# MLP of a two-layer hybrid decoder: the second half of its first part as seven block products

## The chip, the cores and the metric

The kernel runs on one core of one Trainium2 chip. The metric is the device time of one execution in microseconds (us). Before the change the median of three runs is 1323.62 us (1322.04 to 1324.94). All times below are of that core; the engines are TensorE (PE, with its weight loads as PEld), VectorE (DVE), ScalarE (ACT), GpSimd (POOL) and SyncE (SP, which issues most transfers).

## The reference, cut to what matters

Two layers over 512 tokens of width 1024. Each layer has a mixer (attention and an mLSTM, merged and projected by `w_out`) and then an MLP:

```python
def hybrid_layer(x, ..., w_out, norm_ffn, w_ff1, w_ff2):
    ...
    x = x + mixed @ w_out
    u = jax.nn.relu(rmsnorm(x, norm_ffn) @ w_ff1)      # w_ff1: 1024 x 4096
    return x + (u * u) @ w_ff2                         # w_ff2: 4096 x 1024
```

All arrays are float32. The kernel keeps that accuracy by splitting every operand of a large product into a high part `h` (float32 rounded to the matmul's fp32r form, one ACT instruction) and a low part `l` (the rest, one DVE instruction). A product is then three matmuls: high by high, high by low, low by high (`mm3`). The mean square of the norm is not multiplied into the activations but into the MLP's result, so the MLP can begin before the norm's factor is known.

## The kernel before, in words

**Parts.** The MLP's 4096 hidden columns are worked off in four parts. Part p takes the columns 512p to 512p+511 of the lower 2048 and the same of the upper 2048. Within a part, i = 0 and i = 1 take 256 columns each of both (n = 0 lower, n = 1 upper). For every part the first matrix gives `u`, and `second` multiplies it by rows of `w_ff2`.

**Two ways to form `u`.** Parts 1 to 3 use `first`: the activations are cut into four blocks (two halves of the 1024 inputs, two halves of the 512 tokens), the weights into four (two halves of the inputs, n = 0 and 1), and the 2x2 block product is formed with seven block products instead of eight, from sums and differences of blocks. The seven are numbered 1 to 7 and stand in the order 5, 1, 3, 6, 2, 7, 4. One block product is 4 x 2 x 3 = 24 matmuls of 128x128 by 128x256. Its results are copied, added and put through ReLU and square by `copy` (line 1139) and `finish` (lines 1143 to 1145), and the products share banks of PSUM: 5, 3 in one half of the pair of banks "f", 1, 6, 7 in the other half, 2 and 4 in the two small buffers `aux` that the transposes use too. Part 0 uses `Plain`: an ordinary product for each i and n, 8 x 2 x 3 = 48 matmuls of 128x128 by 128x512.

**Differences of the activations.** `left_blocks` forms the sums of high and low again and from them the differences that products 5, 6, 3 and 7 need, splits them and keeps them for all parts (`hs`, and for 7 in the place of a block that is no longer needed, `late`).

**Sums of the weights.** Products 5, 6 and 4 run on growing sums of blocks of `w_ff1`. The buffer `p` is loaded by SP (`w1_load`, line 946) and the next block is added into it by a transfer that accumulates, which only POOL issues (`w1_add`, line 951): one such addition before product 5, one between 5 and 6, one between 6 and 4. Buffer `q` serves 3 and then, after one addition, 7; buffer `r` serves 1 and is loaded anew for 2. Each product's weights are split by `w_split` (ACT line 910, DVE line 911) into one of five pairs of buffers (`SPL = 5`), so a split has to wait until the product five places earlier is done.

**What sets the order.** Each engine works off its own queue in order. The queues are filled by a scheduling layer, which takes the program's order, the marks `high_priority` and `issue_after` and its own picture of durations, and which may put matmuls of one product ahead of another's. `weave` lays side work (transposes of `x`, `norm.turn`, and so on) under a list of matmul groups. While the last product of the mixer runs (`w_out`, splits at lines 192 and 193, additions to `x` at line 879), the MLP's first weights are loaded and split. The transposes of `x` use the two `aux` buffers in turn; each is emptied by ACT (line 207) and DVE (line 208).

Of the kernel before, what the change touches and what calls it, by code (L numbers as in the profile page):

```python
# [35 lines left out]
def hybrid_kernel(ctx, tc, x, norm_mix, w_in, att_q_norm, att_k_norm, att_sinks, m_gate_bias,  # L36
# [25 lines left out]
    def nm(s):  # L62
        uid[0] += 1
        return f"{s}_{uid[0]}"
# [29 lines left out]
    def f32(ap):  # L94
        return ap.bitcast(F32)
# [25 lines left out]
    def g_mix(l, k):  # L121
        return gcol[:, 8 * l + k:8 * l + k + 1]
# [132 lines left out]
    def weave(fill, side=()):  # L255

        side = sorted(side, key=lambda e: e[0])
        at = 0.0
        for width, f in fill:
            while side and side[0][0] <= at + 1e-6:  # L260
                side.pop(0)[1]()
            f()
            at += width
        for _, f in side:
            f()
# [76 lines left out]
    norm = norm0 = Norm(lambda k: g_mix(0, k))  # L342
# [25 lines left out]
    def halves_of(dt=F32):  # L368

        return [half.tile([P, 4, T], dt, tag=f"u{g}", name=nm("u")) for g in range(2)]  # L370
# [515 lines left out]
    def mlp(l, norm, late, phase):  # L886
# [31 lines left out]
        def plus(d, p, q):  # L918
            with tc.high_priority():
                ve.tensor_tensor(d, p, q, op=ALU.add)  # L920
# [8 lines left out]
        def new_u(part):  # L929
            if part % 2:  # L930
                return halves_of()
            return [uraw.tile([P, 4, T], F32, tag=f"u{g}", name=nm("u")) for g in range(2)]
# [24 lines left out]
        starts = []  # L957
# [102 lines left out]
        def left_blocks(temps):  # L1060

            ih, il = norm.big
            views = [t[:, :, H * n:H * (n + 1)] for t in temps for n in range(2)]

            def block(t, k):
                kk, c = slice(4 * k, 4 * k + 4), slice(H * t, H * (t + 1))
                return ih[:, kk, c], il[:, kk, c]

            def whole(r, t, k):
                hi, lo = block(t, k)
                plus(r, f32(hi), f32(lo))
                return r

            def keep(which, r):
                with tc.high_priority():
                    lefts[which] = pieces(r, *(hs.tile([P, 4, H], F32R, tag=f"{n}{which}", name=nm("hs")) for n in "hl"))

            def late():  # L1080
                with tc.high_priority():
                    lefts[7] = pieces(r21, *block(1, 0))

            for which, (t, k) in ((1, (0, 0)), (2, (0, 1)), (4, (1, 1))):
                lefts[which] = block(t, k)
            r22, r12, r11, r21 = views
            whole(r21, 1, 0)
            whole(r22, 1, 1)
            minus(r22, r22, r21)
            keep(5, r22)  # L1090
            whole(r11, 0, 0)
            minus(r22, r22, r11, -1.0)
            keep(6, r22)
            whole(r12, 0, 1)
            minus(r12, r22, r12, -1.0)
            keep(3, r12)
            minus(r21, r11, r21)
            return late

        def first(part, i, u):  # L1100

            c0 = T * part + H * i
            ps = {}

            r = {}

            def load(tag, k, n):
                r[tag] = w1_load(tag, k, n, c0)

            def start():  # L1110
                load("p", 0, 0)
                w1_add(r["p"], 0, 1, c0)

            starts.append(start)

            def weights(which):
                tag = {1: "r", 2: "r", 3: "q", 7: "q"}.get(which, "p")
                if which == 1:
                    load("r", 0, 0)
                elif which == 3:  # L1120
                    load("q", 1, 1)
                elif which == 2:
                    load("r", 1, 0)
                    if starts:
                        starts.pop(0)()
                w = w_split(r[tag])
                more = {5: (1, 1), 6: (1, 0), 3: (0, 1)}.get(which)
                if more:
                    w1_add(r[tag], *more, c0)
                return w  # L1130

            def to(t, n):
                return u[i][:, 2 * n:2 * n + 2, H * t:H * (t + 1)]

            def of(b):
                return ps[b].rearrange("p (m t) -> p m t", m=2)

            def copy(t, n, b):
                sc.activation(to(t, n), of(b), AF.Copy)  # L1139

            def finish(t, n, b):
                z = to(t, n)
                ve.tensor_tensor(z, z, of(b), op=ALU.add)
                sc.activation(z, z, AF.Relu, scale=-1.0 if n else 1.0)
                sc.activation(z, z, AF.Square)

            def slot(which, bank, fresh, *done):

                ws = []

                def run():
                    if fresh:
                        if which == 5:
                            two = banks("f")
                            ps["a"], ps["b"] = two[:, 0, :], two[:, 1, :]
                        elif bank in "cd":
                            ps[bank] = aux()
                    (hi, lo), (ah, al) = ws[0], lefts[which]
                    for m in range(2):
                        c = slice(m * P, (m + 1) * P)  # L1160
                        for kt in range(4):
                            mm3(ps[bank][:, H * m:H * (m + 1)], hi[:, kt, c], lo[:, kt, c], ah[:, kt, :], al[:, kt, :],
                                fresh and m + kt == 0, False, skip_group_check=True)

                def end():
                    with tc.high_priority():
                        for f, t, n in done:
                            f(t, n, bank)

                return Slot([lambda: ws.append(weights(which))], [run], end)  # L1170

            return [slot(5, "b", True, (copy, 1, 1)), slot(1, "a", True, (copy, 0, 0)),
                    slot(3, "b", False, (copy, 0, 1)), slot(6, "a", False, (finish, 0, 1)),
                    slot(2, "c", True, (finish, 0, 0)), slot(7, "a", False, (finish, 1, 1), (copy, 1, 0)),
                    slot(4, "d", True, (finish, 1, 0))]

        class Plain:
# [5 lines left out]
            def load(self, h):  # L1183
                r = w1_load("prpq"[2 * h + self.n], h, self.n, self.i * H)
                self.w[h] = w_split(r)
                if self.i + self.n + h == 3:
                    starts.pop(0)()

            def step(self, k):
                if k == 0:  # L1190
# [9 lines left out]
                    sc.activation(dst, self.ps, AF.Relu)  # L1200
                    sc.activation(dst, dst, AF.Square)

            def slot(self, u):
                return Slot([lambda: self.load(0), lambda: self.load(1)],
                            [lambda h=h: [self.step(k) for k in range(4 * h, 4 * h + 4)] for h in range(2)],
                            lambda: self.evac(u))

        us = [new_u(0)]
        plain = [Plain(0, 0, "f"), Plain(0, 1, "x")]
        for h in range(2):  # L1210
            for f in plain:
                f.load(h)
        weave([(0.5, lambda k=k, f=f: f.step(k)) for k in range(KT) for f in plain],
              late + [(6.5, norm.inverse)])
        for f in plain:
            f.evac(us[0])
        us.append(new_u(1))
        slots = [Plain(1, 0, "y").slot(us[0]), Plain(1, 1, "f").slot(us[0])]
        lates = []
        slots[0].before = lambda: lates.append(left_blocks(us[1]))  # L1220
        for part in range(4):
            nxt = []
            if part < 3:
                if part:
                    us.append(new_u(part + 1))
                nxt = first(part + 1, 0, us[part + 1]) + first(part + 1, 1, us[part + 1])
            two = second(part, us[part])
            if part == 0:
                before = two[1].before
                two[1].before = lambda: (lates.pop()(), before())  # L1230
            for s, n in zip(two, (2, 2, 2, 2, 3, 3, 0)):
                slots += [s] + nxt[:n]
                nxt = nxt[n:]
# [8 lines left out]
        def go(i, s, n):  # L1242
# [16 lines left out]
    late = ([(0.75 + 0.9 * (k - 2), lambda k=k: norm.turn(k)) for k in range(2, KT)]  # L1259
            + [(6.5, lambda: gains(grow, 16))]  # L1260
            + [(3.0 + 2.0 * j, lambda j=j: norm.squares(j)) for j in range(2)])
    order = None
    for l in range(DEPTH):
        with ExitStack() as phase:
            norm = mixer(l, norm, late, order, phase)
        late = norm.steps(1, 1.5, 0.5)
        with ExitStack() as phase:
            norm = mlp(l, norm, late, phase)
        late = norm.steps(0, 1.5, 0.5) if norm else []
# [41 lines left out]
```

## Time and profile before

| | us |
|---|---|
| median of three runs | 1323.62 |
| the profiled execution, whole | 1324.14 |
| its span | 1322.4 |
| PE busy | 1296.7 (98% of the span) |
| DVE busy | 953.9 (72%) |
| ACT busy | 768.4 (58%) |
| POOL busy | 217.9 (16%) |

A row of a timeline reads: start, duration (of all in the row), engine, line, operation, result and operands by the program's names, sizes, count, and in brackets the idle time just ahead and what ended it. Matmuls overlap, so the pace of PE is the distance between starts and not the duration. Rows of DMA show the issue; the time to landing is shown apart. Layer 0's MLP begins at 340.45 us of the span, layer 1's at 994.69 us.

### The profile page before, as it was taken

What the parts mean: (1) busy time and instruction counts of PE and PEld (TensorE: products, weight loads), DVE (VectorE), ACT (ScalarE), POOL (GpSimd) and SP (SyncE); (2) the same over time, 40 slices, a digit from 0 to 9 for tenths busy, and PEclk for the clock granted to TensorE, in tenths of its full rate; (3) what the DMA queues carried; (4) which work ended last, traced back from release to release, by engine and by line L of the source; (5) the groups of instructions that cost most, each with busy time, mean ns of one, the idle gap of its engine ahead of it and who ended that gap; (6) DMA issues with size and microseconds to landing.
All of it is one profiled execution on the core that took longest, in us unless ns stands there. A gap on an engine that the chain in (4) does not pass through costs nothing.

```text
span 1322.4 us, 19224 instructions
## 1 busy us (share of the span) xinstructions
PE 1296.7 (98%) x6966; PEld 1101.0 (83%) x6966; DVE 953.9 (72%) x1493; ACT 768.4 (58%) x1367; POOL 217.9 (16%) x323
## 2 busy tenths in 40 slices
PE   8999999999999999999999999999999999999998
PEld 6877788887889989899788777888888899988987
DVE  4688764466568797978947887645756778879786
ACT  5467765445366655666454687564545566655663
POOL 4422311100001132120005123110000110322100
PEclk9999999999999999999999999999999999999999
DMA  5422236746357989686314222367472589797843
GB/s 152 109 66 75 60 97 153 180 128 218 78 126 187 244 190 236 167 194 194 111 33 120 64 72 64 105 153 174 140 235 66 115 223 251 172 245 149 199 144 128
DMA packets 134400, 192.31 MB, mean 145 GB/s; under 512 B 10264, under 2 KB 71808, under 8 KB 134304
## 3 DMA queue, kind: packets, MB, share of 16 engines
q1 hardware_dynamic: 92768, 135.88, 33.6%
q0 software_dynamic: 33344, 39.98, 19.4%
q10 hardware_dynamic: 8192, 15.21, 3.7%
q8 instruction: 55, 0.90, 0.3%
q14 instruction: 41, 0.34, 0.1%
HBM read 188.95 MB, written 31.46 MB: 167 GB/s over the span
## 4 chain that ended last, share of the span: by engine, by line
PE 48%; DVE 5%; ACT 2%; DMA 2%; issue 1%; DVEq 0%; POOL 0%; SPq 0%; ACTq 0%; POOLq 0%
PE mm L47 42%; PE aux L47 5%; DMA raw<-in_w_ff_dram 1%; PE aux L51 1%; DVE wl L193 1%; DVE wl L911 1%; ACT wh L910 1%; ACT t L652 0%; ACT wh L192 0%; DMA w<-in_w_in_dram 0%; DVE ul L903 0%; DVE x L965 0%; DVE t L639 0%; DVE t L689 0%; DVE t L616 0%
## 5 line engine op out<-in xcount | busy, mean ns | idle before, releaser
L47 PE MATMUL mm<-i,wh 128*128 128x512 f32 (+1 forms) x1280 | 353.6, 362 | 2.2 <-ACT u L1139 2.1
L910 ACT ACTIVATE wh<-raw 128x1024 fp32r<-128x1024 f32 x212 | 223.7, 1056 | 164.5 <-PE mm L47 95.5
L911 DVE TENSOR_TENSOR wl<-raw,wh 128x1024 fp32r<-128x1024 f32 x212 | 257.3, 1220 | 80.1 <-ACT wh L910 79.9
L47 PEld LDWEIGHTS mm<-i,wh 128*128 128x128 f32 x1280 | 224.2, 189 | 36.0 <-ACT u L1139 4.5
L47 PE MATMUL mm<-i,wl 128*128 128x512 f32 (+1 forms) x640 | 230.2, 360 | 0.0
L193 DVE TENSOR_TENSOR wl<-w,wh 128x512 fp32r<-128x512 f32 (+1 forms) x208 | 140.8, 677 | 105.0 <-ACT wh L192 101.2
L192 ACT ACTIVATE wh<-w 128x512 fp32r<-128x512 f32 (+1 forms) x208 | 127.1, 612 | 133.3 <-PE mm L47 99.9
L47 PE MATMUL mm<-wh,ul 128*128 128x512 f32 x448 | 174.8, 390 | 1.1 <-DVE ul L903 1.1
L47 PE MATMUL mm<-wh,uh 128*128 128x512 f32 x448 | 175.1, 391 | 0.0
L47 PE MATMUL mm<-wl,uh 128*128 128x512 f32 x448 | 175.0, 391 | 0.0
L47 PE MATMUL mm<-wh,i 128*128 128x512 f32 (+1 forms) x512 | 149.9, 371 | 0.4 <-ACT wh L192 0.4
L951 POOL DMA_DIRECT2D raw<-in_w_ff_dram x48 | 62.2, 1296 | 522.8 <-DVE wl L911 247.0
L47 PEld LDWEIGHTS mm<-i,wl 128*128 128x128 f32 x640 | 120.9, 189 | 17.6
L47 PE MATMUL mm<-hs,wh 128*128 128x256 f32 x576 | 106.7, 286 | 0.3 <-ACT u L1139 0.3
L47 PEld LDWEIGHTS mm<-wh,i 128*128 128x128 f32 x512 | 92.7, 190 | 16.0 <-ACT wh L192 0.8
L47 PEld LDWEIGHTS mm<-wh,ul 128*128 128x128 f32 x448 | 84.2, 188 | 18.5 <-DVE ul L903 1.6
L47 PEld LDWEIGHTS mm<-wh,uh 128*128 128x128 f32 x448 | 84.3, 188 | 16.4 <-issue 0.2
L47 PEld LDWEIGHTS mm<-wl,uh 128*128 128x128 f32 x448 | 84.3, 188 | 15.7
L47 PEld LDWEIGHTS mm<-hs,wh 128*128 128x128 f32 x576 | 90.1, 191 | 7.5 <-ACT u L1139 6.6
L47 PE MATMUL mm<-wl,i 128*128 128x512 f32 (+1 forms) x256 | 94.8, 370 | 0.0
L965 DVE SCALAR_TENSOR_TENSOR x<-mm,ninv,x 128x512 f32<-128x512 f32 x112 | 80.0, 744 | 16.1 <-PE mm L47 15.6
L47 PE MATMUL mm<-wh,a 128*128 128x512 f32 x256 | 82.1, 394 | 2.3 <-DVE x L879 1.2
(244 smaller groups left out, 2130.5 us busy)
## 6 DMA issues: line engine op xcount, KB each, us to landing
raw<-in_w_ff_dram SPq DMA_DIRECT2D x124, 512.0 KB, 5.1
w<-in_w_in_dram SPq DMA_DIRECT2D x128, 256.0 KB, 2.7
raw<-in_w_ff_dram POOLq DMA_DIRECT2D x48, 512.0 KB, 6.5
sum<-in_w_ff_dram ACTq DMA_DIRECT2D x28, 512.0 KB, 5.0
raw<-sum SPq DMA_DIRECT2D x28, 512.0 KB, 4.2
sum<-in_w_ff_dram POOLq DMA_DIRECT2D x20, 512.0 KB, 6.6
w<-in_w_out_dram SPq DMA_DIRECT2D x32, 256.0 KB, 3.4
w<-in_w_att_branch_dram SPq DMA_DIRECT2D x16, 256.0 KB, 2.6
```

Source lines behind the costliest of these rows:

```text
L47: return nc.tensor.matmul(*args, **kw)
L51: return nc.tensor.transpose(*args)
L192: last_wh[:] = sc.activation(wh[:, :off], raw[:, :off], AF.Copy), wh
L193: ve.tensor_tensor(wl[:, :off], raw[:, :off], f32(wh[:, :off]), op=ALU.subtract)
L910: last_wh[:] = sc.activation(hi, r, AF.Copy), hi[:, 0, :]
L911: ve.tensor_tensor(lo, r, f32(hi), op=ALU.subtract)
L951: nc.gpsimd.dma_start(r, w1_block(k, n, c0), accum_op=ALU.add)
L965: ve.scalar_tensor_tensor(xh[:, i, :], ps[:, i, :], norm.inv[:, 0 if sign > 0 else 1, b:b + 1], xh[:, i, :], op0=ALU.mult, op1=ALU.add)
```

## The change

In part 0 the half i = 0 stays plain, on the banks "x" and "y" instead of "f" and "x". The half i = 1 is formed by `first`, as in parts 1 to 3. `left_blocks` is called within the first half, after the transposes, and its last difference (for product 7) right after that half instead of ahead of a later step of `second`. The start of the first sum of weights is no longer tied to the last plain load: the sum for part 0 starts after the four plain loads, that for part 1 within product 2, as everywhere.

```diff
             def load(self, h):
                 r = w1_load("prpq"[2 * h + self.n], h, self.n, self.i * H)
                 self.w[h] = w_split(r)
-                if self.i + self.n + h == 3:
-                    starts.pop(0)()
...
-            def slot(self, u):
-                return Slot([lambda: self.load(0), lambda: self.load(1)],
-                            [lambda h=h: [self.step(k) for k in range(4 * h, 4 * h + 4)] for h in range(2)],
-                            lambda: self.evac(u))
-
         us = [new_u(0)]
-        plain = [Plain(0, 0, "f"), Plain(0, 1, "x")]
+        plain = [Plain(0, 0, "x"), Plain(0, 1, "y")]
         for h in range(2):
             for f in plain:
                 f.load(h)
+        us.append(new_u(1))
+        slots = first(0, 1, us[0])
+        starts.pop(0)()
+        lates = []
         weave([(0.5, lambda k=k, f=f: f.step(k)) for k in range(KT) for f in plain],
-              late + [(6.5, norm.inverse)])
+              late + [(3.6, lambda: lates.append(left_blocks(us[1]))), (6.5, norm.inverse)])
+        lates.pop()()
         for f in plain:
             f.evac(us[0])
-        us.append(new_u(1))
-        slots = [Plain(1, 0, "y").slot(us[0]), Plain(1, 1, "f").slot(us[0])]
-        lates = []
-        slots[0].before = lambda: lates.append(left_blocks(us[1]))
         for part in range(4):
...
-            if part == 0:
-                before = two[1].before
-                two[1].before = lambda: (lates.pop()(), before())
```

**ACT's queue near the end of the mixer's last product.** `wh<-raw` is the high part of an MLP weight, `wh<-w` of a `w_out` weight, `i<-aux` empties a transpose. Before:

```order
L910 ACTIVATE wh_715_3534<-raw_714_3532 128x1024
L192 ACTIVATE wh_676_3326<-w_675_3324 128x512
L910 ACTIVATE wh_742_3710<-raw_741_3708 128x1024
L192 ACTIVATE wh_683_3360<-w_682_3358 128x512
L192 ACTIVATE wh_688_3392<-w_687_3390 128x512
L192 ACTIVATE wh_691_3414<-w_690_3412 128x512
L207 ACTIVATE i_679_3341<-aux_678_3336,gcol_85 128x512
```

Now:

```order
L910 ACTIVATE wh_715_3534<-raw_714_3532 128x1024
L192 ACTIVATE wh_676_3326<-w_675_3324 128x512
L192 ACTIVATE wh_683_3360<-w_682_3358 128x512
L192 ACTIVATE wh_688_3392<-w_687_3390 128x512
L910 ACTIVATE wh_742_3713<-raw_719_3540 128x1024
L192 ACTIVATE wh_691_3414<-w_690_3412 128x512
L207 ACTIVATE i_679_3341<-aux_678_3336,gcol_85 128x512
```

The fifth weight that is split there was a plainly loaded block (`raw_741`), and it stood two places earlier. It is now the sum for product 5 (`raw_719`), a load and an accumulating transfer after it; behind it stand a `w_out` split and the first transpose's high part. DVE's low part of it has moved in the same way, behind the additions to `x`.

**PE's queue where the second half begins.** `mm_756` is the pair of banks "f", `aux_769` the buffer of product 2, `aux_777` that of product 4. Before, the half begins as 24 matmuls on one weight:

```order
L47 MATMUL mm_718_3545<-i_679_3341,wh_715_3534 128x512
L47 MATMUL mm_718_3545<-i_680_3342,wh_715_3534 128x512
L47 MATMUL mm_718_3545<-i_679_3341,wl_716_3535 128x512
L47 MATMUL mm_758_3744<-i_679_3341,wh_742_3710 128x512
L47 MATMUL mm_758_3744<-i_680_3342,wh_742_3710 128x512
L47 MATMUL mm_758_3744<-i_679_3341,wl_743_3711 128x512
```

Now (24 matmuls of product 5, ten of product 2, then product 1):

```order
L47 MATMUL mm_756_3745<-hs_727_3629,wh_742_3713 128x256
L47 MATMUL mm_756_3745<-hs_726_3628,wl_743_3714 128x256
L47 MATMUL aux_769_3875<-i_679_3341,wh_754_3741 128x256
L47 MATMUL aux_769_3875<-i_680_3342,wh_754_3741 128x256
L47 MATMUL aux_769_3875<-i_679_3341,wl_755_3742 128x256
...
L47 MATMUL mm_756_3745<-i_679_3341,wh_745_3720 128x256
L47 MATMUL mm_756_3745<-i_680_3342,wh_745_3720 128x256
L47 MATMUL mm_756_3745<-i_679_3341,wl_746_3721 128x256
```

Ten matmuls of product 2 stand between products 5 and 1, its other fourteen behind product 1; pieces of product 4 stand between 1 and 3, 3 and 6, 6 and 7. Product 2's split weights are `wh_754` and `wl_755`.

**ACT's queue under the end of the first half and the start of the second.** `hs` are high parts of differences (5, 6, 3 in this order), `i<-u` that of difference 7, lines 1200 and 1201 before and 1198 and 1199 now are ReLU and square of the plain half. Before:

```order
L902 ACTIVATE hs_735_3691<-u_725_3678 128x1024
L902 ACTIVATE hs_737_3697<-u_725_3678 128x1024
L910 ACTIVATE wh_751_3728<-raw_750_3726 128x1024
L902 ACTIVATE hs_739_3703<-u_725_3678 128x1024
L1200 ACTIVATE u_703_3512<-mm_717_3538 128x1024
L910 ACTIVATE wh_756_3739<-raw_754_3735 128x1024
L1200 ACTIVATE u_703_3512<-mm_718_3545 128x1024
```

Now:

```order
L902 ACTIVATE hs_726_3628<-u_717_3538 128x1024
L902 ACTIVATE i_679_3341<-u_718_3539 128x4x256
L902 ACTIVATE hs_728_3634<-u_717_3538 128x1024
L910 ACTIVATE wh_750_3731<-raw_719_3540 128x1024
L1198 ACTIVATE u_703_3512<-mm_720_3543 128x1024
L902 ACTIVATE hs_730_3640<-u_717_3538 128x1024
L910 ACTIVATE wh_754_3741<-raw_752_3736 128x1024
L1198 ACTIVATE u_703_3512<-mm_721_3550 128x1024
L910 ACTIVATE wh_757_3771<-raw_747_3724 128x1024
L1139 ACTIVATE u_704_3513<-mm_756_3745 128x2x256
```

The high part of difference 7 is new at this place, between those of 5 and 6. From difference 6 on there are, in a row, product 6's weight, a ReLU, difference 3, product 2's weight, a ReLU, product 7's weight and the copy of product 5's result. DVE's queue has the low part of difference 7 ahead of the step that makes difference 6, and product 2's low part behind that of difference 3.

## The prediction

> **What bounds the kernel now.** First the page: the busy shares. Then PE's waits in the stretch that the change touches in layer 0.
>
> ```profile
> span 1322.4 us, 19224 instructions
> PE 1296.7 (98%) x6966; PEld 1101.0 (83%) x6966; DVE 953.9 (72%) x1493; ACT 768.4 (58%) x1367; POOL 217.9 (16%) x323
> ```
>
> ```profile
> PE mm L47 <- ACT u L1139: 1.0, 1, 1.0
> PE mm L47 <- DVE x L879: 1.0, 1, 1.0
> ```
>
> PE is the bound: it idles only 2 us between 316 and 400 us. So a matmul less is a gain of its whole pace, and any work on ACT, DVE, POOL or the transfers costs nothing until PE stands for it. The prediction is therefore a sum of two things: matmul time saved, and new stops of PE.
>
> **The products.** Next PE's timeline in layer 0: first and last row of the plain second half, then one whole block product of part 1, and the stop behind it.
>
> ```profile
> 364.18 0.62 PE L47 MATMUL mm<-i,wh 128*128 128x512 f32 x2
> ...
> 385.94 0.39 PE L47 MATMUL mm<-wh,uh 128*128 128x512 f32 x1
> ...
> 391.38 0.40 PE L47 MATMUL mm<-hs,wh 128*128 128x256 f32 x2
> 391.62 0.28 PE L47 MATMUL mm<-hs,wl 128*128 128x256 f32 x1
> ...
> 394.25 0.40 PE L47 MATMUL mm<-wh,uh 128*128 128x512 f32 x1
> ...
> 395.93 0.50 PE L47 MATMUL mm<-i,wh 128*128 128x256 f32 x2 [1.05 <-ACT u L1139]
> ```
>
> The plain half takes 385.94 - 364.18 = 21.76 us for 96 matmuls. A block product takes 394.25 - 391.38 = 2.87 us for 24, so seven take 20.09. The change saves 1.67 us per layer, not an eighth of 21.76 (2.72), because a matmul of 256 columns takes 0.120 and not half of 0.227. [...]
>
> The last row shows the price of the form: the banks of products 5 and 1 are one buffer, and product 1 stood 1.05 us until ACT (line 1139) had copied product 5's result. In the changed queue ten matmuls of product 2 are put there as cover. So what counts is whether product 2's weights are ready when product 5 ends.
>
> **The stop at product 2.** ACT and DVE at the end of the first half, and ACT's later copy for its duration:
>
> ```profile
> 361.59 1.06 ACT L902 ACTIVATE hs<-u 128x1024 fp32r<-128x1024 f32 x1 [4.71 <-DVE u L927]
> 362.80 1.07 ACT L910 ACTIVATE wh<-raw 128x1024 fp32r<-128x1024 f32 x1
> 363.76 1.04 ACT L902 ACTIVATE hs<-u 128x1024 fp32r<-128x1024 f32 x1
> 364.71 1.01 ACT L1200 ACTIVATE u<-mm 128x1024 f32<-128x1024 f32 x1
> 365.62 1.05 ACT L910 ACTIVATE wh<-raw 128x1024 fp32r<-128x1024 f32 x1
> 366.56 1.01 ACT L1200 ACTIVATE u<-mm 128x1024 f32<-128x1024 f32 x1
> ...
> 395.30 0.58 ACT L1139 ACTIVATE u<-mm 128x512 f32<-128x512 f32 x1
> ```
>
> ```profile
> 359.07 1.22 DVE L903 TENSOR_TENSOR hs<-u,hs 128x1024 fp32r<-128x1024 f32 x1
> 360.33 1.23 DVE L927 SCALAR_TENSOR_TENSOR u<-u,u 128x1024 f32<-128x1024 f32 x1
> 361.59 1.23 DVE L927 SCALAR_TENSOR_TENSOR u<-u 128x1024 f32<-128x1024 f32 x1
> ...
> 382.71 1.22 DVE L903 TENSOR_TENSOR i<-u,i 128x1024 fp32r<-128x1024 f32 x1
> ```
>
> Two things are to be seen. The differences were already formed under the first half before: DVE's rows from 359 to 363 lie ahead of 364.18. Calling them "under the first half" moves one pair only, that of difference 7 (382.71 on DVE). And that pair now stands ahead of difference 6, at the one place where ACT waits for DVE (4.71 us). DVE's steps of this size follow each other by some 1.2 us (359.07, 360.33, 361.59, each with a small one between; 1.14 without, as 315.54 and 316.68 below), so the high part of difference 6 moves from 361.59 to 362.7. From there ACT has eight instructions without a gap, 0.95 apart ((366.56 - 362.80) / 4): difference 6, weight 6, ReLU, difference 3, weight 2, ReLU, weight 7, copy of 5. Weight 2's high part ends at 362.7 + 4 x 0.95 + 1.06 = 367.6. On DVE its low part follows that of difference 3 (whose high part ends at 362.7 + 3 x 0.95 + 1.04 = 366.6), so it starts at 366.6 + 1.14 = 367.8 and ends at 369.0. The copy ends at 362.7 + 7 x 0.95 + 0.58 = 369.9.
>
> PE ends product 5 at 364.2 + 2.87 = 367.05. Product 2's first two matmuls need the high part (stop of 0.55), the third the low part: PE stands again, 1.1 us, to 369.0. Eight more take 1.0: product 1 begins at 370.1 instead of 367.05 + 10 x 0.12 = 368.25. Cost **1.85 us** per layer. Were the weight ready, the copy alone would still hold product 1 to 369.9. I add 0.2 for restarts: a first pair after a stop takes 0.34 (395.93 to its follower) instead of 0.24 (391.38 to 391.62), two such here. The later products' splits and additions (three weights more than the plain half had, 1.06 on ACT and 1.22 on DVE each, seven short copies, ReLUs and squares) lie under 18 us of PE work; by the same steps each is done within 0.1 us of its need. Without that cover they would cost some 2.3 us per weight.
>
> **The moved split.** SP, ACT, DVE and PE near the end of the mixer, and ACT's same split in layer 1:
>
> ```profile
> 309.38 1.89 SPq L946 DMA_DIRECT2D raw<-in_w_ff_dram  x2
> ```
>
> ```profile
> 314.44 1.06 ACT L910 ACTIVATE wh<-raw 128x1024 fp32r<-128x1024 f32 x1 [3.50 <-DMA raw<-in_w_ff_dram]
> ...
> 968.70 1.06 ACT L910 ACTIVATE wh<-raw 128x1024 fp32r<-128x1024 f32 x1 [2.70 <-DMA raw<-in_w_ff_dram]
> ```
>
> ```profile
> 315.54 1.23 DVE L911 TENSOR_TENSOR wl<-raw,wh 128x1024 fp32r<-128x1024 f32 x1 [3.87 <-ACT wh L910]
> 316.68 1.28 DVE L879 TENSOR_TENSOR x<-x,mm 128x512 f32<-128x512 f32 x2
> 317.88 0.68 DVE L193 TENSOR_TENSOR wl<-w,wh 128x512 fp32r<-128x512 f32 x1
> 318.48 0.68 DVE L879 TENSOR_TENSOR x<-x,mm 128x512 f32<-128x512 f32 x1
> ...
> 322.27 0.75 DVE L208 SCALAR_TENSOR_TENSOR i<-aux,gcol,i 128x512 fp32r<-128x512 f32 x1 [1.19 <-ACT i L207]
> ```
>
> ```profile
> 318.01 0.50 PE L47 MATMUL mm<-wh,a 128*128 128x512 f32 x1 [0.99 <-DVE x L879]
> ...
> 324.57 0.60 PE L51 MATMUL aux<-ident,x 128*128 128x128 f32 x4
> ```
>
> The fifth weight lands at 314.4 (split at 314.44). Its DVE half at 315.54 is what made the addition to `x` late and PE stand 0.99; moved behind these additions, that stop goes. But the weight is now the sum for product 5: after the load POOL has to add the second block, and ACT and DVE wait for it in order, with a `w_out` split and the first transpose behind them. The third transpose (324.57, without the old stop 323.58) reuses the first one's buffer and waits for DVE's emptying. If the addition takes A from POOL's issue, it lands at 314.5 + A; DVE's low part starts 1.10 later (314.44 to 315.54), the `w_out` low part 1.14 after that, the emptying 0.60 after that (317.88 to 318.48), and takes 0.75: 314.5 + A + 3.6. PE's new stop is A - 5.4, and with the old one gone the step costs **A - 6.4** per layer. Layer 1 has the same pattern (968.70 - 314.44 = 654.26, the distance between the two MLPs to 0.03).
>
> What is A? Rows of POOL's accumulating transfers with their time to landing, and the engines and transfers (last two columns: share, GB/s) in the stretch in question:
>
> ```profile
> 325.68 1.34 POOL L951 DMA_DIRECT2D raw<-in_w_ff_dram  x1 [70.05 <-PE aux L51]
> DMA to landing us min/median/max: 11.9/11.9/11.9
> ...
> 361.16 1.28 POOL L951 DMA_DIRECT2D raw<-in_w_ff_dram  x1 [34.13 <-DMA raw<-in_w_ff_dram]
> DMA to landing us min/median/max: 6.1/6.1/6.1
> ...
> 421.28 1.28 POOL L951 DMA_DIRECT2D raw<-in_w_ff_dram  x1 [19.81 <-DVE wl L911]
> DMA to landing us min/median/max: 6.9/6.9/6.9
> ```
>
> ```profile
> 316.00:319.00 3.00, 2.01 (x9) 1.36 (x8) 3.00 (x5) 0.55 (x2) 0.00 (x0) 1.00 0.03 11
> ...
> 322.00:325.00 3.00, 3.00 (x19) 2.47 (x18) 2.10 (x3) 1.45 (x3) 0.00 (x0) 1.00 1.01 341
> ```
>
> Undisturbed it is 6.1; behind five loads 11.9; with two loads and another addition around it 6.9. At 314.5 the transfers were nearly idle before (share 0.03 from 316), but the change fills that gap: the second sum's addition follows on POOL 1.3 us later, and a `w_out` load and product 1's weight, which SP issued at 318 to 319, go out some 4 us earlier, since the DVE step that frees their buffer is no longer late. That is nearest to the row with 6.9 and a little fuller. I take A = 7.3, and keep 6.1 and 11.9 as its ends: the step costs 0.9 (-0.3 to 5.5). [...]
>
> **The sum.** Per layer -1.67 + 1.85 + 0.2 + 0.9 = +1.3, for two layers **+2.6 us**. Nothing else on PE's path changes: the parts behind have the same products, and the old stop at 395.93 stands as it did. The profiled execution would be 1324.14 + 2.6 = 1326.7; it lies 0.5 above the median shown, so the median to expect is 1323.62 + 2.6 = **1326.2 us**, 0.2% up.
>
> **The rivals.**
> 1. *The addition lands in a crowd* (A of 9 to 12, as at 325.68). Then ACT's queue stands, and the transposes behind it: 2 x (11.9 - 6.4 + 0.4) = +11.8, 1335.4 us; with A = 9, +6, 1329.6. For it: two additions and three loads go out within 3 us. Against it: the loads at 325.68 were five, with 2.5 MB still to go. Decides from A = 8.5.
> 2. *Faster: PE never stands at the second half.* If weight 2 is split by 367.05 and the copy done by 368.25, about 1.9 us earlier than worked out, the 1.85 goes, and with A = 6.1 the sum is 2 x (-1.67 - 0.3) = -3.9, 1319.7 us. For it: in parts 1 to 3 the same products run with almost no stop. Against it: there other products stand between them, here ACT has eight instructions in a row for them.
> 3. *The change does only half of this:* one of the two stops shows, the other not (A near 6.1, or ACT ahead of its row): with A = 6.1, 2 x (-1.67 + 1.85 + 0.2 - 0.3) = +0.2; with weight 2 in time, 2 x (-1.67 + 0.9) = -1.5: 1322.1 to 1323.8 us, no difference that shows. For it: each stop rests on one chain of its own. Against it: the chains are of rows that repeat in both layers.
>
> **How the numbers follow.** The forecast with both stops has 0.70, the crowd 0.12, the faster case 0.10, the half case 0.08. A difference under 0.2% (2.65 us) is about what a measurement of this kernel can't tell from none. The forecast lies on that line: half of it (0.36) is above with A over 7.3, the rest (0.34) below. So slower by over 0.2%: 0.36 + 0.12 = 0.48; within: 0.34 + 0.08 = 0.42; faster: 0.10. The range runs from 1322.2 (half case) to 1331.0 (A up to 9.7); it leaves out the faster case and the worst of the crowd.
>
> **What would show it.** PE in the second half of layer 0: a stop of 0.5 and one of about 1.1 ahead of `aux<-i,wh` and `aux<-i,wl` (256 columns), released by ACT (line 910) and DVE (line 911), and else 20 us of block products without a gap. Near the mixer's end: no stop for DVE's addition to `x`, and a stop of about 1.9 ahead of the third group of transposes, released by DVE's emptying; ACT idle for some 5 us ahead of the sum's split, waiting for a transfer. POOL's first addition at 314.5 with 6.1 to 9 us to landing. The prediction is wrong if that addition lands after 10 us, if PE runs on through product 2, or if a stop appears in parts 1 to 3 that is not there now.

## The result, and the profile after

The changed kernel takes 1339.44 us (median of four runs, 1338.49 to 1340.71), the kernel before 1324.28 in the same set: ratio 1.0119, 95% interval 1.0107 to 1.0130, so 15.2 us slower. Forecast were 1326.2 us and a range to 1331.0. The direction was right, the size was not.

Head of the page, then PE's waits from 300 to 400 us:

```profile
span 1336.8 us, 19580 instructions
PE 1300.5 (97%) x7110; PEld 1109.9 (83%) x7110; DVE 966.4 (72%) x1507; ACT 780.5 (58%) x1389; POOL 225.2 (17%) x331
```

```profile
PE aux L51 <- DVE i L208: 3.7, 1, 3.7
PE aux L47 <- DVE wl L911: 1.0, 1, 1.0
PE aux L47 <- ACT wh L910: 0.3, 1, 0.3
```

In this stretch the stops stand where the prediction put them, and no others. Yet PE is also 3.8 us *busier* than before (1300.5 against 1296.7), with less matmul work. That is the first sign that something beside waiting costs time. The starts of the same pieces of work on PE's timeline show where the 14.4 us of the two spans come from:

| PE begins | before | after | difference | added by this stretch |
|---|---|---|---|---|
| `w_out`, ahead of the transposes | 314.60 | 314.40 | -0.20 | |
| layer 0: plain half | 340.45 | 345.58 | 5.13 | **5.33** |
| layer 0: second half | 364.18 | 369.19 | 5.01 | -0.12 |
| layer 0: `second` | 385.94 | 391.44 | 5.50 | **0.49** |
| layer 0: last stretch of `second` | 619.73 | 626.75 | 7.02 | **1.52** |
| layer 1: plain half | 994.69 | 1007.86 | 13.17 | **6.15** |
| layer 1: second half | 1018.41 | 1031.52 | 13.11 | -0.06 |
| layer 1: `second` | 1040.17 | 1053.76 | 13.59 | **0.48** |
| layer 1: last stretch of `second` | 1274.09 | 1288.46 | 14.37 | **0.78** |

The half with seven block products costs 0.49 and 0.48 us, about as forecast (0.38). The loss lies in two other places: near the mixer's end (5.33 and 6.15, forecast 0.9), and in the later parts (1.52 and 0.78, forecast nothing).

**Near the mixer's end.** ACT, DVE and POOL with the landing of POOL's transfer, then PE:

```profile
323.28 1.06 ACT L910 ACTIVATE wh<-raw 128x1024 fp32r<-128x1024 f32 x1 [7.14 <-DMA raw<-in_w_ff_dram]
...
326.12 0.74 DVE L208 SCALAR_TENSOR_TENSOR i<-aux,gcol,i 128x512 fp32r<-128x512 f32 x1
...
314.16 1.34 POOL L951 DMA_DIRECT2D raw<-in_w_ff_dram  x1 [58.73 <-PE mm L47]
DMA to landing us min/median/max: 9.1/9.1/9.1
```

```profile
322.81 0.39 PE L47 MATMUL mm<-wh,a 128*128 128x512 f32 x1
326.92 1.11 PE L51 MATMUL aux<-ident,x 128*128 128x128 f32 x4 [3.71 <-DVE i L208]
...
332.86 0.39 PE L47 MATMUL mm<-wl,a 128*128 128x512 f32 x1
333.09 0.63 PE L47 MATMUL mm<-wh,a 128*128 128x512 f32 x2
```

The accumulating transfer lands 9.1 us after its issue, at 323.26; the split starts there, DVE empties the first transpose 2.9 later, and the third transposes start at 326.92 after a stop of 3.71. Then PE runs slowly. For the third and fourth transposes and the eleven matmuls of 512 columns among them, from 326.92 to 333.09, it takes 6.17 us. The same amount of work in the kernel before (there its second and third transposes and eleven matmuls):

```profile
322.74 0.60 PE L51 MATMUL aux<-ident,x 128*128 128x128 f32 x4
...
326.16 0.39 PE L47 MATMUL mm<-wh,a 128*128 128x512 f32 x1
```

That is 3.42 us, so 2.75 us are lost while PE counts as busy. Stretches of the changed kernel (columns: stretch, its length, busy time and count for PE, PEld, DVE, ACT, POOL, then granted clock, DMA share, GB/s):

```profile
322.00:326.90 4.90, 1.20 (x6) 0.64 (x4) 2.53 (x4) 3.25 (x5) 1.01 (x1) 0.90 0.74 124
326.90:332.10 5.20, 5.18 (x17) 4.31 (x18) 2.66 (x4) 1.94 (x4) 0.28 (x1) 0.50 0.89 205
332.10:334.00 1.90, 1.90 (x8) 1.57 (x7) 1.76 (x2) 1.84 (x6) 0.00 (x0) 0.83 1.13 278
```

The granted clock is 0.50 for over five microseconds behind the stop. Layer 1 shows the same (stop of 3.89, 0.50 from 989.2 to 994.5, 2.67 us lost).

**In part 2.** First the kernel before, then the changed one: POOL with the landing of the addition (line 951; line 402 is a helper transfer that adds up rows of `w_ff2`), ACT and PE:

```profile
464.71 1.30 POOL L951 DMA_DIRECT2D raw<-in_w_ff_dram  x1 [8.03 <-DVE wl L911]
DMA to landing us min/median/max: 6.1/6.1/6.1
470.47 1.81 POOL L400 COPY mark<-wh 1x2 f32<-1x2 f32 x1 [4.46 <-ACT wh L910]
```

```profile
468.19 0.95 POOL L402 DMA_DIRECT2D sum<-in_w_ff_dram  x1 [0.28 <-issue]
471.04 1.33 POOL L951 DMA_DIRECT2D raw<-in_w_ff_dram  x1 [1.90 <-DVE wl L911]
DMA to landing us min/median/max: 10.8/10.8/10.8
...
481.96 1.06 ACT L910 ACTIVATE wh<-raw 128x1024 fp32r<-128x1024 f32 x1 [2.12 <-DMA raw<-in_w_ff_dram]
482.92 0.58 ACT L1139 ACTIVATE u<-mm 128x512 f32<-128x512 f32 x1
...
483.55 0.50 PE L47 MATMUL mm<-i,wh 128*128 128x256 f32 x2 [1.53 <-ACT u L1139]
```

A helper transfer stands ahead of the addition now. The addition lands late, product 6's split waits for it, and the copy of product 5, for which PE's product 1 waits, is queued behind that split.

### The profile page after: what moved, and what is told of

The parts are those of the page before. It is cut to its first block, busy times and chain, and to the rows that moved or that the text cites. A ratio compares the mean times of both kernels' runs of the same rounds, so it can differ in the third digit from the quotient of the medians.

```text
span 1336.8 us, 19580 instructions
## 1 busy us (share of the span) xinstructions
PE 1300.5 (97%) x7110; PEld 1109.9 (83%) x7110; DVE 966.4 (72%) x1507; ACT 780.5 (58%) x1389; POOL 225.2 (17%) x331
## 5 line engine op out<-in xcount | busy, mean ns | idle before, releaser
L47 PE MATMUL mm<-i,wh 128*128 128x512 f32 (+1 forms) x1216 | 325.7, 355 | 4.5 <-ACT u L1139 4.3
L910 ACT ACTIVATE wh<-raw 128x1024 fp32r<-128x1024 f32 x218 | 230.0, 1056 | 159.5 <-PE mm L47 85.6
L911 DVE TENSOR_TENSOR wl<-raw,wh 128x1024 fp32r<-128x1024 f32 x218 | 264.5, 1220 | 68.9 <-ACT wh L910 68.6
L47 PEld LDWEIGHTS mm<-i,wh 128*128 128x128 f32 x1216 | 210.2, 189 | 33.7 <-ACT u L1139 6.7
L47 PE MATMUL mm<-i,wl 128*128 128x512 f32 (+1 forms) x608 | 214.2, 352 | 0.0
L951 POOL DMA_DIRECT2D raw<-in_w_ff_dram x56 | 72.7, 1298 | 511.1 <-DVE wl L911 271.8
L47 PEld LDWEIGHTS mm<-i,wl 128*128 128x128 f32 x608 | 115.0, 189 | 15.1
L47 PE MATMUL mm<-hs,wh 128*128 128x256 f32 x672 | 124.4, 286 | 0.2
L47 PEld LDWEIGHTS mm<-hs,wh 128*128 128x128 f32 x672 | 105.2, 191 | 7.8 <-ACT u L1139 6.7
L47 PE MATMUL mm<-hs,wl 128*128 128x256 f32 x336 | 94.9, 283 | 0.0
```

The source lines that it names most:

```text
L47: return nc.tensor.matmul(*args, **kw)
L910: last_wh[:] = sc.activation(hi, r, AF.Copy), hi[:, 0, :]
L911: ve.tensor_tensor(lo, r, f32(hi), op=ALU.subtract)
L951: nc.gpsimd.dma_start(r, w1_block(k, n, c0), accum_op=ALU.add)
```

## The experiments

Ratios are to the kernel before, measured in the same set, with 95% intervals; the changed kernel has 1.0119. The edits are shown in short: words in angle or round brackets and behind # stand for code that is not printed here.

### What the stop costs: four runs

*The split held back.* The split of product 5's sum goes behind the fourth transpose in the queues of ACT and DVE.

```diff
-                w = w_split(r[tag])
+                w = w_split(r[tag], (norm.hi[3], norm.lo[3]) if (part, i, which) == (0, 1, 5) else ())
+    (w_split issues its two instructions behind those given)
```

> The changed kernel, with only the split of product 5's sum (ACT and DVE) put behind the mixer's fourth transpose in both queues; the additions and every other order stay. Theory: that split makes the emptying of the first transpose wait for the accumulating transfer, PE stands 3.7 and 3.9 us, and the half clock behind that (about 2.75 us a layer) comes from the standing still. Then both go: 1339.4 - 2 x (3.9 + 2.75) = about 1326. Rival A, the half clock has another cause and stays: 1339.4 - 7.8 = 1331.6. Rival B, the wait comes back at the additions to x or at product 5, PE stops 2 us or more elsewhere: 1330 or above.

Measured: 1325.46 us, ratio 1.0017 (1.0007 to 1.0027). The stop is gone, and what the mixer's end had cost with it. In the traced execution (1323.47 us) PE runs through that stretch at full clock:

```profile
317.00:330.00 13.00, 13.00 (x67) 10.79 (x66) 9.00 (x11) 8.18 (x17) 0.70 (x1) 1.00 1.13 305
```

This one place in two queues was worth 13 us of the 15.

*Useless work in the stop.* 16, 8 and 4 matmuls on zeros ahead of the third transposes.

```diff
+        pad = lambda: [pe.matmul(<current sum>, zeros, <current weight>, start=False, stop=False) for _ in range(16)]
-                  norm.steps(0, 1.5, 0.5) if j else [])
+                  norm.steps(0, 1.5, 0.5) + [(2.499, pad)] if j else [])
```

> The changed kernel, with 16 matmuls of 128x512 on a weight of zeros (they add nothing to the sum they go to) ahead of the third transpose in both layers, where PE stands 3.7 and 3.9 us. Theory: standing still is what halves the clock; the added 16 x 0.227 = 3.6 us of work lie in the stop and cost nothing, the clock stays full: 1339.4 - 2 x 2.75 = 1333.9. Rival: the clock is halved by something else (the transfers, the transposes): the same time as the changed kernel, 1339.4, with a granted clock of 0.5 behind the stop as before.

> As the run with 16, with 8 matmuls on zeros: PE still stands 3.9 - 1.8 = 2.1 us. Theory: a stop of 2.1 us is too short to halve the clock (in the kernel before a stop of 1.5 us left it at 1.000): 1333.9 as with 16. Rival: any stop over 2 us halves it: 1339.4, with 0.5 in the granted clock behind it.

> As the runs with 16 and 8 matmuls on zeros, with 4: PE stands about 3.0 us. [...]

Measured: 1333.13 us with 16 (1.0075, 1.0060 to 1.0090), 1335.89 with 8 (1.0098, 1.0082 to 1.0115), 1338.39 with 4 (one run). With 16, PE's timeline and a stretch:

```profile
321.79 3.83 PE L47 MATMUL mm<-wh,zeros 128*128 128x512 f32 x16
326.32 0.66 PE L51 MATMUL aux<-ident,x 128*128 128x128 f32 x4 [0.70 <-DVE i L208]
```

```profile
326.30:331.60 5.30, 5.28 (x27) 4.46 (x28) 4.49 (x7) 3.83 (x9) 0.28 (x1) 1.00 0.84 204
```

3.8 us of useless work per layer made the kernel 6 us faster, since it kept the clock: standing still is what halved it. With 8 the stops were 2.21 and 2.54, and in the traced execution (1334.00 us) the clock stayed full too. It did not in all four: two took 1337.2 and 1337.5 us at a mean granted clock of 0.998 and 0.997. With 4 PE stood 2.93 in layer 0, as expected, but 4.18 in layer 1, and half a clock followed both. Stretches around the 2.93:

```profile
326.90:327.90 1.00, 0.98 (x6) 0.88 (x7) 1.00 (x2) 0.29 (x1) 0.28 (x1) 0.83 0.59 133
327.90:328.50 0.60, 0.60 (x3) 0.48 (x2) 0.39 (x2) 0.40 (x1) 0.00 (x0) 0.50 0.80 184
...
330.00:331.00 1.00, 1.00 (x6) 1.00 (x5) 0.25 (x1) 0.69 (x2) 0.00 (x0) 0.51 1.11 308
331.00:332.00 1.00, 1.00 (x6) 0.78 (x6) 0.78 (x2) 1.00 (x2) 0.00 (x0) 1.00 1.22 222
```

PE resumed at full clock, fell to half about 0.6 us later, and was back at 331. So 2.93 us was enough here, and the fall can come after the stop.

### Why the transfer took 9.1 us: two runs

*The second addition moved back.* Part 1's first addition (316.10) goes behind the third one in POOL's queue.

```diff
-                w1_add(r["p"], 0, 1, c0)
+                w1_add(r["p"], 0, 1, c0, adds[1:2] if (part, i) == (1, 0) else ())
```

> The changed kernel, with only the first accumulating transfer of part 1's sum (issued 1.9 us behind the first one at 314.16) moved behind the third in POOL's queue. Theory: two accumulating transfers at once share POOL's queue, so the first takes 9.1 us instead of 6.1; alone it lands after 6.1 to 7.0, PE's stop falls from 3.7 to 0.7 to 1.6 us, too short for the half clock: 1339.4 - 2 x (2.6 + 2.75) = 1328.7 (1327 to 1330). Rival: the loads that SP has under way are the crowd; it still takes 8.5 or more, the stop stays above 3 us, 1337 to 1339.

Measured: 1337.59 us, ratio 1.0107 (1.0092 to 1.0122). The first transfer still took 9.1 us, and PE's stops were 4.99 and 4.58, so the theory of two additions that share POOL's queue fell, and the rival stood.

*SP's 512 KB loads moved back as well.*

```diff
                 elif which == 1:
+                    if (part, i) == (0, 1): w_marks[:] = w_loads[-1:] * 4   # behind the last w_out load
                     load("r", 0, 0)
```

> As the run with the second addition moved back, and SP's three loads of 512 KB that it issues beside the first accumulating transfer (product 1's weight at 314.61, product 3's, part 1's first) put behind the mixer's last w_out load. Theory, since the second addition turned out not to matter: the 512 KB loads under way are what makes the accumulating transfer take 9.1 us; without them it lands after 6.1 to 7.5, PE's stop of 5.0 us falls to 2.0 to 3.4 and the half clock goes: 1337.6 - 2 x (1.6 to 3.0 + 2.75) = 1326 to 1329. Rival: the w_out loads (256 KB each, they stay) are enough, or the transfer takes 9 us after a load in any case: 8.5 or more, 1335 to 1338.

Measured: 1331.82 us, ratio 1.0057 (1.0043 to 1.0072). POOL's first addition with its landing, and PE's stop:

```profile
L951 POOL DMA_DIRECT2D raw<-in_w_ff_dram x1: 1344/1344/1344, 315.8 to 315.8; - x1
DMA to landing us min/median/max: 6.2/6.2/6.2
```

```profile
325.58 0.66 PE L51 MATMUL aux<-ident,x 128*128 128x128 f32 x4 [1.36 <-DVE i L208]
```

So SP's 512 KB loads were the crowd: 6.2 us without them (two of 256 KB still ran beside it), and the clock stays full there. Of the three loads named, SP's timeline of the changed kernel has two beside the addition, product 1's (314.61, 6.4 us to landing) and the tail of part 1's; product 3's went out only at 326.6. The time lies 3 us above the expectation; in layer 1 product 1 of part 1 then stood 2.40 us, with half a clock behind it. Loads that are moved back are late elsewhere.

### The second half: two runs

*Difference 7 formed late*, on top of the held split.

```diff
-        lates.pop()()
+        slots[3].before = lambda: lates.pop()()      # and behind product 2's split, on ACT and DVE
```

> As the run with the held split, and difference 7's high and low part formed behind product 2's weight split instead of ahead of difference 6 (and 20 matmuls of product 2 stand between products 5 and 1 now, 10 before). Theory: the step at its early place delays ACT's chain by 1.1 us, and product 2's stops (0.26 and 0.97) are the price; now at most 0.6 of stop is left there and the second half takes about 21.0 us and not 22.25: 1325.5 - 2 x 1.2 = 1323.1. Rival: the stop comes back ahead of product 1, which waits for the copy of product 5 behind the same ACT instructions: 1325.5.

Measured: 1325.29 us, ratio 1.0010 (1.0001 to 1.0018). From the start of the half to part 1's product 5 PE took 27.80 us, against 27.72 in the changed kernel and 27.20 before: no gain. The stops came back as 0.52 ahead of product 2's low part and 0.55 ahead of product 4's weight; the rival stood, at another product than named.

*The plain half's ReLUs and squares behind the copy of product 5*, on top of that.

```diff
-        for f in plain:
-            f.evac(us[0])
+        slots[2].before = lambda: [f.evac(us[0]) for f in plain]     # and behind the copy, on ACT
```

> The run with the held split and the late difference 7, and the plain half's two ReLUs and squares put behind the copy of product 5 in ACT's queue (they stood ahead of it: product 2's split one ReLU and the copy two ReLUs later). Theory: the second half takes 22.3 us instead of 20.1 because ACT has more work queued ahead of what PE needs than PE's work covers, whichever step is moved; with two steps of 0.95 taken out of that chain product 2's weight is ready at 366.9 of the old count (needed 367.3) and product 4's at 372.7 (needed 372.8), so the half takes 20.3 to 20.8: 1325.3 - 2 x 1.7 = 1321.9. Rival: the stop moves on again, to product 4's weight behind the ReLUs: 1324 to 1325.

Measured: 1325.03 us, ratio 0.9999 (0.9990 to 1.0008). The same stretch took 26.58 us, 1.14 less than in the changed kernel and 0.62 less than the plain form; no wait of PE that the profile lists is left in the half. So ACT's queue had kept that much of the saving from showing. It is still not the 1.67 of the prediction: unbroken, the stretch would take 20.09 + 5.44 = 25.53, and pauses too short to be listed hold the other 1.05. Only part of the gain reached the end: the stop ahead of product 1 in part 1 grew to 1.50 and 1.82.

### The stops in the later parts: six runs

*The copy of product 5 ahead of product 6's split* in parts 1 to 3: for both i on top of the late difference 7, then for i = 0 alone on top of the held split, and for i = 0 in the kernel before.

```diff
-                w = w_split(r[tag])
+                w = w_split(r[tag], [r["copy"]] if part and which == 6 else ())     # issued after the copy
```

> As the run before it (held split, late difference 7), and in parts 1 to 3 ACT copies product 5's result ahead of the split of product 6's sum, which waits for an accumulating transfer, instead of behind it. Theory: the stops ahead of product 1 in parts 1 to 3 (1.56, 0.88, 1.04, 0.62 in the run with the held split) are that copy queued behind a split whose data is late; they go but for 0.2 or so each: 1323.1 - 3.5 = 1319.6, below the kernel before. Rival: product 6 itself stands for its weight then, as long as product 1 did: 1323.

> The run with the held split, and the copy of product 5 ahead of product 6's split in parts 1 to 3 for i = 0 alone (for both i it cost 27 us: for i = 1 the split starts the next accumulating transfer, which then came late for 7 to 9 us of stop each). Theory: the stops of 1.56 and 0.88 (layer 0) and 1.04 and 0.62 (layer 1) ahead of product 1 go but for some 0.2 each, less 0.7 of cover that moves away: 1325.5 - 2 to 3 = 1322.5 to 1323.5, no slower than the kernel before. Rival: product 6 stands for its weight as long: 1325.5.

> The kernel before, with the same edit of the copy and nothing else. If the stop ahead of product 1 in the kernel before (1.05 in each layer) is that copy in ACT's queue behind the split, and no more: 2 x 0.85 = 1.7 us below the kernel before. If the split is then late instead: no difference.

Measured: 1352.10 us (1.0215, 1.0178 to 1.0252), 1348.30 us (1.0184, 1.0147 to 1.0220), and 1321.64 us in the kernel before (0.9983, 0.9974 to 0.9991). The kernel before with the edit, ACT and PE in part 1:

```profile
394.34 0.60 ACT L1139 ACTIVATE u<-mm 128x512 f32<-128x512 f32 x1 [1.78 <-PE mm L47]
394.83 1.05 ACT L910 ACTIVATE wh<-raw 128x1024 fp32r<-128x1024 f32 x1
...
394.99 0.50 PE L47 MATMUL mm<-i,wh 128*128 128x256 f32 x2 [0.22 <-ACT u L1139]
```

The old stop of 1.05 was the copy's place in the queue. In the other two runs that stop fell to 0.22 as well, but stops of 7 to 10 us appeared in parts 2 and 3. The reading that i = 1 was to blame fell with the second of them. Its executions spread from 1341.31 to 1355.66 us, and what spreads them is open; POOL and DVE in the longest, which was traced:

```profile
475.81 7.96 POOL L400 COPY mark<-wh 1x2 f32<-1x2 f32 x1 [10.12 <-ACT wh L910]
483.72 0.61 POOL L402 DMA_DIRECT2D sum<-in_w_ff_dram  x1
484.31 2.68 POOL L951 DMA_DIRECT2D raw<-in_w_ff_dram  x2
```

```profile
475.70 1.21 DVE L920 TENSOR_TENSOR raw<-raw,raw 128x1024 f32<-128x1024 f32 x1
...
481.38 2.35 DVE L911 TENSOR_TENSOR wl<-raw,wh 128x1024 fp32r<-128x1024 f32 x2
483.65 1.40 DVE L965 SCALAR_TENSOR_TENSOR x<-mm,ninv,x 128x512 f32<-128x512 f32 x2
```

A POOL instruction of two elements stands 7.96 us, from just after DVE begins a row of seven instructions with both inputs in SBUF (475.70) to 0.12 us after DVE begins the first with an input from PSUM (483.65). The additions queued behind it on POOL start only at 484.31. In the changed kernel an instruction of the same line took 0.17 us at 467.74, where DVE stood idle, and 1.87 at 479.97, beside two such instructions of DVE, to 0.12 us after the first with an input from PSUM (481.72). No run here tells why.

*The ReLUs behind the copy, and the copy first in part 1 alone*, where POOL has no such instruction:

> As the run before it, and in part 1 for i = 0 alone the copy of product 5 ahead of the split of product 6's sum (in parts 2 and 3 that edit let a small POOL instruction stand 8 us and cost 23 us; part 1 has no such instruction). Theory: the stop of 1.05 to 1.56 ahead of product 1 there falls to 0.2, as the same edit showed in the kernel before: 1321.9 - 2 x 0.9 = 1320.1, 0.25% below the kernel before. Rival: the split that is 0.5 later starts the next addition later and PE stands for it: 1322 or above.

Measured: 1322.11 us, ratio 0.9985 (0.9976 to 0.9995): less than the theory's 0.25%, but faster than both kernels.

*The helper transfers at their old places.* They start at every fourth step of a list that the change made three steps longer at its front.

```diff
-            if i % 4 == 1:
+            if i > 3 and i % 4 == 0:
                 beat()
```

> The run with the held split, and the helper transfers that add up rows of w_ff2 (line 402 on POOL, line 397 on ACT) started three steps later in the list of steps. They start at every fourth step counted from the start of that list, and the change made the list three steps longer at its front, so they all moved against the parts. Theory: that is what put a sum ahead of part 2's second addition in POOL's queue, so that this addition lands after 10.8 us instead of 6.1 and PE stands 1.5 us more ahead of product 1 (1.5 us in layer 0, 0.8 in layer 1); with the old places the parts take what they took before: 1325.5 - 2.3 = 1323.2, ratio to the kernel before 1.000. Rival: the addition is late because of the loads around it: the stop stays, 1325.5, ratio 1.0017.

> All repairs together: held split, late difference 7, ReLUs behind the copy, the copy of product 5 ahead of product 6's split for i = 0 in parts 1 to 3, and the helper transfers at their old places. Theory: POOL's small instruction stood 8 us in parts 2 and 3 because it became free just as DVE began a row of instructions with both inputs in SBUF; at the old places it does not meet that row (in the kernel before with the same copy edit it took 2.1 us): ratio about 0.997, some 1320. Rival: the 8 us come again: 1340 or more.

Measured: with the held split 1327.68 us (1.0023, 1.0011 to 1.0035); with all repairs 1321.20 us (0.9978, 0.9969 to 0.9986). In the first, part 2's addition landed after 7.4 us and product 1 no longer stood there, as the theory says; but in part 1 an addition took 10.3 us and product 1 stood 2.15 and, in layer 1, 2.44, so the total did not fall. In the second, POOL's small instruction took 1.81 us and no stop of 8 us came. All repairs together make the seven-product form 0.22% (2.9 us) faster than the kernel before. But they include the copy's new place, which alone brought the kernel before to 1321.64 us (0.9983), and the two intervals overlap; without it, and with the helper transfers where the change put them, the repaired form was even (0.9999). So no run shows that seven products in this half are faster in themselves.

## Why the prediction was wrong, point by point

**What bounds the kernel: right.** Every microsecond lost is PE standing, or PE slow.

**The products and the stop at product 2: right.** Forecast -1.67, stops of 0.55 and 1.1 and a net of +0.38; measured stops of 0.25 and 0.96 and a net of +0.49 and +0.48. The sum is nearer than its parts, and that is partly luck: from start to start product 2's delays take 1.74 us in layer 0 where 2.05 were forecast, and pauses under the later products, which the prediction put at nothing, add some 0.4. That ACT's chain sets the stops was shown by taking two steps out of it (26.58 us against 27.80 in the run without that edit). The sub-step that blamed difference 7 was at most a part: moving it alone gained nothing in this stretch.

**The moved split: the mechanism right, A mis-sized.** The formula for the stop, A - 5.4 (the rows it is added up from give A - 5.5), makes it 3.7 for A = 9.1; measured 3.71. But A was taken as 7.3, from the row with 6.9; the 512 KB loads beside the addition, product 1's half a microsecond behind it and the tail of part 1's, were good for some 3 us more (9.1 with them, 6.2 without; no run takes product 1's away alone). That is 1.8 us in layer 0 and, with 9.0, 1.7 in layer 1, where the stop of 3.89 is 0.3 over the formula. The sentence that layer 1 "has the same pattern" was wrong for the old stop: it was 0.99 in layer 0 but 0.2 in layer 1, so 0.8 less was won back there.

**A missing term: the price of a stop.** The sum counted a stop at its own length. A stop of 3.7 us costs its length and 2.75 us more at half a clock (2.67 in layer 1), 5.4 us in two layers. The same fault is in the first rival: its condition came true (A of 9), at 1339.4 us and not at its 1329.6. Shorter stops can have such a price: half a clock followed those of 2.40, 2.44 and 2.93 in other runs.

**"Nothing else on PE's path changes": wrong.** The helper transfers are counted by steps of the list that the change lengthened, so they moved against the additions in the later parts: 1.52 and 0.78 us where nothing was forecast, among it the stop of 1.53 in part 2, a stop of the kind that the prediction itself named as a sign of being wrong. The run at the old places shows it for the stop in part 2, and also that putting them back alone gains nothing, since a stop in part 1 grows instead; why the addition there then takes 10.3 us is left open.

The parts: 2.6 forecast, + 3.5 (A) + 0.8 (old stop of layer 1) + 5.4 (clock) + 0.2 (second half) + 2.3 (later parts) = 14.8, against 14.4 between the spans. The range had room for the first two of these (to 1330.5 us) and not for the clock.

## What to carry to other kernels

A stop of the bounding engine is not a number to be added alone: ask what its clock does behind it (here half a clock behind one of 3.71 us, and 2.75 us more lost). Where several engines are queued behind one transfer, the place of the waiting instruction in each queue decides, and moving it by a few places was worth 13 us here with all work unchanged. And look in the program for what is counted by position (every fourth step of a list): an edit at the front of the list moves it everywhere behind. And give a repair to the old form too before its gain is put down to the new one.

## What the runs showed of the hardware

**Stops that halve the clock.** Half a clock followed the stops of 3.71 and 3.89 in the changed kernel, of 4.99 in the run with the second addition moved back, of 2.93 and 4.18 in the run with 4 matmuls on zeros, of 2.40 in the run with SP's loads moved back as well, and of 2.44 in layer 1 of the run with the held split and the old helper places. The clock stayed full behind those of 2.21 and 2.54 in the run with 8 matmuls, of 2.15 in layer 0 of the run with the old helper places, and of 1.53, the longest in the kernel before. So length alone doesn't decide. In the changed kernel the clock fell at 325.93 and at 988.11, 662.18 us apart, and stood at half for 6.82 and 6.83 us; in the run with the old helper places it was back after 3.41. The 6.82 is twice that, and 662.18 is 194 times 3.413. With the changed kernel cut into steps of that length, counted from its falls, PE stood 2.72 us in the step ahead of each of the two, and at most 1.53 in any step behind which the clock stayed full. In the kernel before, cut into such steps from the fall at its end (1323.06), it was at most 1.47, with the clock full throughout. (The first 20 us and the last 7 of a span are left out.) One step and what followed for the stop of 3.71, that of 2.44, and that of 2.54:

```profile
322.51:325.92 3.41, 0.69 (x4) 0.22 (x2) 1.55 (x2) 2.64 (x5) 0.03 (x1) 1.00 0.88 142
325.93:332.75 6.82, 5.83 (x18) 4.86 (x19) 4.18 (x7) 3.19 (x7) 1.25 (x1) 0.50 0.79 183
...
1049.96:1053.37 3.41, 1.44 (x13) 1.24 (x11) 3.41 (x5) 1.12 (x2) 0.00 (x0) 1.00 0.29 94
1053.37:1056.78 3.41, 2.94 (x13) 2.94 (x14) 3.41 (x4) 1.36 (x2) 1.97 (x2) 0.50 0.00 0
...
984.43:987.84 3.41, 1.91 (x11) 1.61 (x12) 3.20 (x6) 1.80 (x4) 1.28 (x1) 1.00 0.29 67
987.84:991.25 3.41, 3.41 (x19) 2.85 (x18) 2.80 (x5) 3.18 (x9) 0.00 (x0) 1.00 1.02 243
```

In the first row PE works 0.69 of 3.41 us and so stands 2.72; in the third it stands 1.97; in the fifth 1.50, since the stop of 2.54 lies across two steps. Of the six stops named between 2 and 3 us three had half a clock behind them. No run here tests whether such a step is the cause.

**POOL's queue kept the transfer engines longer per byte.** From the page of the kernel before (queue, packets, MB, share of 16 engines):

```profile
q1 hardware_dynamic: 92768, 135.88, 33.6%
q0 software_dynamic: 33344, 39.98, 19.4%
```

That is 0.25% of the engines' time per MB on SP's queue and 0.49% on POOL's, where nearly all bytes are transfers that accumulate: half a megabyte there took as much packet time as a whole one on SP's. No run here tells whether the accumulating or the queue is the reason.
